# Other sources, orders and queues around the same matmuls: the first block's 1/rms from feature tiles, sums cast a step later, stores moved between two DMA queues

## The chip, the cores and the metric

The kernel runs on one core of one Trainium2 chip. The metric is the device time of one execution in microseconds (us); the time of a kernel is the median of its runs. TensorE is called PE, VectorE DVE, ScalarE ACT, GpSimd POOL, and SyncE, which here only starts transfers, SP.

## The reference

One layer of a hybrid network runs over 2048 prompt tokens and 64 sample tokens, 2112 rows of 1024 features in fp32. Cut to what matters here:

```
h    = rms_norm(x, g_pre)
vA, bA, cA, zA, q, f, iv, zB, gA, gB = split(h @ w_in)            # ten blocks of 1024 columns
yA   = (silu(zA) * bA * conv3(cA * vA)) @ w_a_out
o    = gated linear recurrence over q, f, iv, in chunks of 64 tokens, 8 heads
yB   = (rms_norm(o) * g_onorm * silu(zB)) @ w_b_out
x    = x + rms_norm((sigmoid(gA) * yA + sigmoid(gB) * yB) @ w_o, g_post)
x    = x + (p @ w_ple_proj) * sigmoid(rms_norm(x, g_ple) @ w_ple_gate)
```

`rms_norm(x, g)` is x / sqrt(mean(x*x) + 1e-6) * g over the 1024 features of a token. What the change calls W_G is `w_ple_gate`, and "ple" is the product of p (256 features) with `w_ple_proj`.

## The kernel before

**Tiles and products.** Features lie on the 128 partitions and tokens along the free dimension, so x comes as eight feature tiles `x_fm[k]` of 128 x 704. The tokens are done in three blocks of 704, each as two halves of 352 columns. Every fp32 product is made of three matmuls: each operand is split into a rounded part hi (a cast on ACT) and the rest lo (a subtraction on DVE) by `split` (L188), and hi*hi, hi*lo and lo*hi are added in PSUM. Most pairs of weight column blocks go through `sgroup`, which multiplies sums and differences of weight blocks (S1 to S4) with sums and differences of activation halves (T1 to T4), seven products (n = 0 to 6) in place of eight. `hook()` runs one queued step of other work after each product.

**The start (L1263 to L1370).** SP's queue asks for everything in this order: p of block 0, the ple weights (raws), the rows of block 0 as token tiles `x_tok` (twelve loads of 128 x 512), p of block 1, one feature tile of x, four weight tiles, the seven other feature tiles. ACT and DVE square and add up the twelve row tiles; GpSimd's power (L592) makes 1/rms, and six transposes (`spread`, L603) lay it out along the tokens as `rs`. PE meanwhile does block 0's ple, eight steps j of twelve matmuls (L1043 to L1045). Instructions are held in a written order by `behind_all` (behind named instructions on their engines) and `placed` (behind the last matmul).

Then `first_operands` (L702) makes the operands of block 0, one feature tile k at a time: `scaled_x` (L684, DVE) multiplies x by the gain and `rs`, `split` makes hi and lo, and from k = 4 on `sums_of` (L666) forms the four differences of the pair k-4, k (L670 to L673, DVE) and splits them at once into hi and lo. Two steps run ahead; the others are interleaved by `next_k` with block 1's ple (one step j, twelve matmuls, evacuated by ACT at L1050) and with the first `plain_group` (L432 to L434, twelve matmuls for each k). A second `plain_group` follows, whose weight splits are placed behind the entries of `summed`, and after it the first `sgroup` that needs the T sums.

**Stored sums.** A group's S sums and lo parts are made once (`combined`, L286), stored to DRAM by SP (`keep_sum` L276, `split_w` L225), and loaded again by the later blocks (L198, L219). Two groups are not formed in block 0, because `plain_group` did their columns there: FF/QQ of head 0 and the last GB group. They are formed at the start of block 1, and their sums stored by SP as well. The tag `s` has three buffers, which hold both new sums and some reloaded lo parts (`low_tile`).

**Heads.** `path_b` does a head with two `sgroup`s (FF/QQ and ZB/IV), and from the second head on with one gate group behind them; the head's attention steps are then put in the list of hooks and run within the next groups. For head 0 of block 0 there is no gate group, so its hooks start with the next product.

**The end.** In the last block `final_norm` runs once for each half, as hooks within the last product. It loads x again by GpSimd (`fetch`, L1176), two tiles ahead, normalizes (L1185, L1186), squares on ACT (L637), adds up on DVE (L638); the column sums are matmuls with ones (L619). The gate product of block 1 (`final_gate` with W_G, L528 to L530) was postponed into the last block and runs there in the same stretch; it reloads x and p by GpSimd (L1066), multiplies and adds (L1219, L1220) and stores y by GpSimd (L1221).

Of the kernel before, what the change touches and what calls it, by code (L numbers as in the profile page):

```python
# [10 lines left out]
F32 = mybir.dt.float32  # L11
# [71 lines left out]
def hybrid_step(  # L83
# [126 lines left out]
    def sum_tile(dt=F32):  # L210
        return wp.tile([P, 4, P], dt, tag="s", name=nm("s"), bufs=3)

    def split_w(raw, key=None):

        hi = wp.tile([P, 4, P], F32R, tag="hi", name=nm("hi"))
        if key in lows:
            lo = low_tile()
            A.copy(hi, raw)  # L218
            SP.dma_start(lo.bitcast(F32), lows[key])  # L219
            return hi, lo  # L220
        lo = wp.tile([P, 4, P], F32R, tag="lo", name=nm("lo"))
        split(raw, hi, lo)
        if key is not None:
            lows[key] = dram.tile([P, 4, P], F32, tag=f"lo{key}", name=nm("low"), bufs=1)
            SP.dma_start(lows[key], lo.bitcast(F32))  # L225
        return hi, lo

    def load_w(idx, anew=False):
# [41 lines left out]

    sums = {}

    def keep_sum(name, i1, s):

        sums.setdefault(i1, {})[name] = dram.tile([P, 4, P], F32, tag=f"{name}_{i1}", name=nm(name), bufs=1)
        SP.dma_start(sums[i1][name], s)  # L276
        return split_w(s, (i1, name))

    def kept_w(i1, i2, name, anew=False):

# [4 lines left out]

    def combined(i1, i2, first):  # L286

        with tc.high_priority():
            if not first:
                return {n: kept_w(i1, i2, n) for _, n, _, _, _ in PRODUCTS}  # L290
            a11, a21, a22, a12 = (load_raw(w_blk[i, h]) for i, h in ((i1, 0), (i2, 0), (i2, 1), (i1, 1)))
            out = dict(A11=split_w(a11, (i1, 0)))

            def total(name, x, y, op):
                s = sum_tile()
                V.tensor_tensor(s, x, y, op)
                out[name] = keep_sum(name, i1, s)
# [5 lines left out]
            out["A12"] = split_w(a12, (i1, 1))  # L303
            out["A22"] = split_w(a22, (i2, 1))
            total("S4", a12, s2, ALU.subtract)
            return out

# [40 lines left out]
    def sgroup(i1, i2, hc, sink, first, mid=None, by_k=False):  # L348


        w = combined(i1, i2, first or i1 not in sums)
        ps, got = {}, {}

        def product(n, ks):
            bank, block, operand, start, _ = PRODUCTS[n]
            if bank not in ps:
                ps[bank] = ps_gemm()
            hi, lo = w[block]
            for k in ks:
                xhi, xlo = hc[operand][k]  # L360
                add = partial(T.matmul, ps[bank], skip_group_check=not start)
                add(hi[:, k, :], xhi, start=start and k == 0, stop=False)  # L362
                add(hi[:, k, :], xlo, start=False, stop=False)  # L363
                last[0] = add(lo[:, k, :], xhi, start=False, stop=k == KH - 1).ins  # L364

        if by_k:
            for k in range(KH):
                for n in range(4):
                    product(n, (k,))
        for n, (bank, _, _, _, stop) in enumerate(PRODUCTS):  # L370
            if n >= 4 or not by_k:
                product(n, range(KH))
            if not stop:
                got[n] = hf()
                with tc.high_priority():
                    copied = A.copy(got[n], ps[bank])  # L376
                copies[0] = copied.ins
                if n == 2 and mid is not None:
                    mid(copied.ins)
            if n == 3:  # L380
                u2 = got[0]
                adds[0] = V.tensor_tensor(u2, u2, ps["b"], ALU.add).ins
            elif n == 4:
                sink(0, 0, ps["a"], None)
            elif n == 5:
                sink(1, 0, u2, ps["c"])
                adds[0] = V.tensor_tensor(got[1], got[1], got[2], ALU.add).ins
                sink(1, 1, u2, got[1])
# [313 lines left out]
    def first_operands(hc, rs, xs, hs):  # L702


        ends = []
        for k in range(KB):
            with behind_all(ends[k - 2][1:] if k >= 2 else ()):
                scaled_x(xs[k], k, rs)
# [4 lines left out]
            else:  # L713
# [285 lines left out]
    def path_b(bl, hc, first, kept, fills, hs):  # L999
# [6 lines left out]
        for hd in range(NH):  # L1006
# [157 lines left out]
    def final_norm(bl, segs, xo, acc, h2, kept, raw=False):  # L1164
# [10 lines left out]
                xks.append(rt())  # L1175
                G.dma_start(xks[j][:, c], x_fm[j * P : (j + 1) * P, segs[0]["t0"] : segs[0]["t0"] + n])  # L1176

        for _ in range(2 if bl["last"] else 4):
            fetch()
        copy = V.tensor_copy if bl["last"] else A.copy  # L1180
        yield from rms(acc, rs, segs, copy)
# [23 lines left out]
                h2[j] = None  # L1205
            yield

    def final_gate(bl, segs, h2, kept):
        def fetch(j):
            return [reload(kept[kind, j]) for kind in "xp"] if j < KB else None  # L1210

# [1 line left out]
        for j in range(KB):  # L1213
# [4 lines left out]
                A.activation(t[:, cols_of(s)], ps, AF.Sigmoid)  # L1218
            V.tensor_tensor(t, pj, t, ALU.mult)  # L1219
            V.tensor_tensor(t, t, xj, ALU.add)  # L1220
            G.dma_start(y_fm[j * P : (j + 1) * P, bl["t0"] : bl["t0"] + BN], t)  # L1221
            yield

    def rows_again(kept, h2):
# [42 lines left out]
    with tc.high_priority():  # L1267
        ph0 = load_p(blocks[0], SP)
        raws = [rt(4 * P).rearrange("p (j k c) -> p j k c", j=2, c=P) for _ in range(KH)]
        raws = [raw[:, j] for raw in raws for j in range(2)]  # L1270
        rows, xs, w1 = [], [], {}
        places = [(s["t0"] + o, q * 512) for s in blocks[0]["segs"] for _, o in tiles_of(HN) for q in range(2)]

        def ask_ple(*js):
            for j in js:
                SP.dma_start(raws[j], w_ple[j])

        def ask_rows(n):
            for r, c in places[len(rows) : len(rows) + n]:
                rows.append(rt(512))  # L1280
                SP.dma_start(rows[-1], x_tok[r : r + P, c : c + 512])

        def ask_x(n):
            for k in range(len(xs), len(xs) + n):
# [16 lines left out]
        ask_x(7)  # L1301
        held = []

        def held_split(j):
# [14 lines left out]
    ss = small.tile([P, 2, 6], F32, tag="rows", name="rows", bufs=1)  # L1319
    for n in range(4):  # L1320
        with behind_all(done):
            for i in range(3 * n, 3 * n + 3):
                t, total = rows[i], ss[:, i % 2, i // 2 : i // 2 + 1]
                if i % 3 == 2:
                    V.tensor_tensor(t, t, t, ALU.mult)
                    V.tensor_reduce(total, t, axis=mybir.AxisListType.X, op=ALU.add)
                else:
                    A.activation(t, t, AF.Square, accum_out=total)
            if n == 3:
                V.tensor_tensor(ss[:, 0, :], ss[:, 0, :], ss[:, 1, :], ALU.add)  # L1330
                done = [*done, rstd_of(ss[:, 0, :], ss[:, 0, :], 1.0 / D)]
# [10 lines left out]
    for _ in range(2):  # L1342
        with placed():
            run(first_ple, 1)
# [25 lines left out]
    for bi, bl in enumerate(blocks):  # L1370
# [125 lines left out]
```

## Time and profile before

| | |
|---|---|
| median of 3 runs | 2632.4 us (2630.19 to 2634.68) |
| the profiled execution | 2636.6 us; its span 2634.9 us |
| busy, share of the span | PE 99%, DVE 63%, ACT 58%, POOL 15% |
| mean granted PE clock | 0.995 |
| moved by DMA | 749.14 MB, mean 284 GB/s |

The span runs from the first to the last instruction, and 1.7 us of the execution lie around it. Times within the trace are counted from the span's start. In a row of the timeline stand the start, the duration, the engine, the line, the operation, result and operands, the shapes and a count; in brackets the engine's idle time before it and what ended that. The granted clock is a share of full speed.

### The profile page before, as it was taken

Reading aid. Unit: us, or ns where it says so; the run is one execution under the profiler, and the core shown is the slowest. Engines: PE = TensorE matmul, PEld = TensorE weight load, DVE = VectorE, ACT = ScalarE, POOL = GpSimd, SP = SyncE. Lnnn points to the kernel's source line nnn. Section 1 sums busy time; section 2 is a strip of 40 time slices with the busy share of each in tenths; the row PEclk is TensorE's granted clock in tenths of the full one; section 3 lists DMA queues with packets and bytes.
Section 4 is the critical chain, followed back from the end, with each engine's and each line's share of the span. In section 5 each row is a group of like instructions: output and inputs, shape, how many; then the busy total and the mean of one; then the engine's idle time right before and its main releaser. Section 6 shows DMA issues by size and latency. Waiting matters only on the chain.

```text
span 2634.9 us, 47400 instructions
## 1 busy us (share of the span) xinstructions
PE 2600.3 (99%) x16550; PEld 2582.7 (98%) x16550; DVE 1666.3 (63%) x3233; ACT 1538.5 (58%) x2948; POOL 386.9 (15%) x713
## 2 busy tenths in 40 slices
PE   7999999999999999999999999999999999999999
PEld 7999999999999999999999999999999999999998
DVE  7687887898777555455545568553455544479656
ACT  5666666554334644677745556466667745565636
POOL 1000000200432210011112211021000101210220
PEclk9999999999999999999999999999999999999999
DMA  8678778898988997767789989599777789989967
GB/s 290 220 262 283 246 269 278 298 316 291 332 299 283 350 328 257 244 224 226 223 288 358 386 306 313 187 363 346 230 228 222 223 258 345 379 308 308 329 234 240
DMA packets 364912, 749.14 MB, mean 284 GB/s; under 512 B 44832, under 2 KB 49472, under 8 KB 364672
## 3 DMA queue, kind: packets, MB, share of 16 engines
q1 hardware_dynamic: 322560, 584.00, 65.2%
q0 software_dynamic: 41824, 162.06, 16.8%
q8 instruction: 130, 2.13, 0.3%
q14 instruction: 110, 0.90, 0.1%
q10 hardware_dynamic: 288, 0.05, 0.0%
HBM read 534.88 MB, written 211.04 MB: 283 GB/s over the span
## 4 chain that ended last, share of the span: by engine, by line
PE 92%; DMA 3%; DVE 2%; issue 1%; ACT 1%; POOL 0%; SPq 0%; ACTq 0%; DVEq 0%; POOLq 0%
PE pg L362 19%; PE pg L364 19%; PE pg L363 19%; PE pg L529 5%; PE pg L530 5%; PE pg L528 5%; PE pg L495 4%; PE pg L496 4%; PE pg L497 4%; PE pa L980 1%; PE pa L944 1%; PE pa L982 1%; PE pa L930 1%; DMA raw<-S 1%; DMA r<-x_fm 1%
## 5 line engine op out<-in xcount | busy, mean ns | idle before, releaser
L362 PE MATMUL pg<-r,hi 128*128 128x352 f32 x3304 | 1094.8, 331 | 4.2 <-DVE r L408 2.6
L363 PE MATMUL pg<-r,hi 128*128 128x352 f32 x3304 | 1068.0, 323 | 0.0
L364 PE MATMUL pg<-r,lo 128*128 128x352 f32 x2356 | 763.2, 324 | 2.2 <-DMA lo<-low 2.2
L218 ACT CAST hi<-raw 128x512 fp32r<-128x512 f32 x720 | 444.3, 619 | 498.8 <-PE pg L363 167.3
L362 PEld LDWEIGHTS pg<-r,hi 128*128 128x128 f32 x3304 | 623.0, 189 | 9.0 <-DVE r L408 4.0
L363 PEld LDWEIGHTS pg<-r,hi 128*128 128x128 f32 x3304 | 623.3, 189 | 0.0
L364 PEld LDWEIGHTS pg<-r,lo 128*128 128x128 f32 x2356 | 443.6, 188 | 2.9 <-DMA lo<-low 2.8
L364 PE MATMUL pg<-r,s 128*128 128x352 f32 x948 | 307.2, 324 | 0.0
L529 PE MATMUL pg<-r,hi 128*128 128x352 f32 x768 | 249.5, 325 | 0.0
L528 PE MATMUL pg<-r,hi 128*128 128x352 f32 x768 | 249.3, 325 | 0.1
L188 ACT CAST hi<-raw 128x512 fp32r<-128x512 f32 x218 | 134.3, 620 | 152.9 <-PE pg L363 46.1
L188 DVE TENSOR_TENSOR r<-r,r 128x352 fp32r<-128x352 f32 (+3 forms) x298 | 183.1, 636 | 63.8 <-ACT r L188 62.9
L496 PE MATMUL pg<-r,hi 128*128 128x352 f32 x672 | 217.3, 325 | 0.0
L495 PE MATMUL pg<-r,hi 128*128 128x352 f32 x672 | 213.6, 325 | 0.1
L530 PE MATMUL pg<-r,lo 128*128 128x352 f32 x656 | 213.0, 325 | 0.0
L188 ACT CAST r<-r 128x352 fp32r<-128x352 f32 (+3 forms) x298 | 161.9, 578 | 61.9 <-DVE r L671 17.4
L188 DVE TENSOR_TENSOR lo<-raw,hi 128x512 fp32r<-128x512 f32 x218 | 149.3, 686 | 68.1 <-ACT hi L188 59.3
L364 PEld LDWEIGHTS pg<-r,s 128*128 128x128 f32 x948 | 178.6, 188 | 0.0
L188 ACT CAST hi<-s 128x512 fp32r<-128x512 f32 x160 | 98.1, 619 | 123.8 <-PE pg L363 112.8
L376 ACT COPY hf<-pg 128x352 f32<-128x352 f32 x354 | 157.0, 446 | 12.2 <-PE pg L364 11.6
L529 PEld LDWEIGHTS pg<-r,hi 128*128 128x128 f32 x768 | 145.2, 189 | 0.4 <-DVE r L188 0.3
L528 PEld LDWEIGHTS pg<-r,hi 128*128 128x128 f32 x768 | 145.1, 189 | 0.4 <-ACT r L188 0.4
(372 smaller groups left out, 4160.5 us busy)
## 6 DMA issues: line engine op xcount, KB each, us to landing
raw<-w_blk SPq DMA_DIRECT2D x570, 256.0 KB, 4.2
lo<-low SPq DMA_DIRECT2D x411, 256.0 KB, 4.4
raw<-S SPq DMA_DIRECT2D x408, 256.0 KB, 4.4
low<-lo SPq DMA_DIRECT2D x322, 256.0 KB, 3.7
s<-low SPq DMA_DIRECT2D x309, 256.0 KB, 4.2
S<-s SPq DMA_DIRECT2D x160, 256.0 KB, 3.1
r<-w_blk POOLq DMA_DIRECT2D x64, 256.0 KB, 7.2
S<-r POOLq DMA_DIRECT2D x64, 256.0 KB, 5.9
```

What stands on the lines that cost most here:

```text
L188: return A.copy(hi, src).ins, V.tensor_tensor(lo, src, hi.bitcast(F32), ALU.subtract).ins
L218: A.copy(hi, raw)
L362: add(hi[:, k, :], xhi, start=start and k == 0, stop=False)
L363: add(hi[:, k, :], xlo, start=False, stop=False)
L364: last[0] = add(lo[:, k, :], xhi, start=False, stop=k == KH - 1).ins
L376: copied = A.copy(got[n], ps[bank])
L495: add(hi[:, k, :], xhi, start=start and k == 0, stop=False)
L496: add(hi[:, k, :], xlo, start=False, stop=False)
L497: last[0] = add(lo[:, k, :], xhi, start=False, stop=k == KH - 1).ins
L528: T.matmul(ps, hi[:, k % 4, :], xhi[:, c], start=k == ks[0], stop=False)
L529: T.matmul(ps, hi[:, k % 4, :], xlo[:, c], start=False, stop=False)
L530: last[0] = T.matmul(ps, lo[:, k % 4, :], xhi[:, c], start=False, stop=k == ks[-1]).ins
```

## The change

Six things change. (1) Block 0's rows are not loaded as token tiles any more. SP's order is p, two ple weights, two tiles of x, and so on, then p of block 1 and the four weight tiles. ACT squares the eight feature tiles, DVE adds them up, and the sums over the partitions are six matmuls with ones (`col_rstd`), as in the later norms. (2) `sums_of` is cut in two: a pair's differences are formed in its own step, behind the split of that step's x, and their casts are made one step later, with a last step for the last pair. (3) The hooks of head 0 in block 0 start three products later. (4) The sums that block 1 forms are stored by GpSimd in place of SP. (5) The last block's `final_norm` loads x three tiles ahead in place of two. (6) The postponed W_G product stores y by SP in place of GpSimd.

```
-    def split_w(raw, key=None):
+    def split_w(raw, key=None, queue=SP):
...
-            SP.dma_start(lows[key], lo.bitcast(F32))
+            queue.dma_start(lows[key], lo.bitcast(F32))
...
-    def keep_sum(name, i1, s):
+    def keep_sum(name, i1, s, queue):
...
-        SP.dma_start(sums[i1][name], s)
-        return split_w(s, (i1, name))
+        queue.dma_start(sums[i1][name], s)
+        return split_w(s, (i1, name), queue)
...
     def combined(i1, i2, first):
+        queue = SP if first else G
         with tc.high_priority():
-            if not first:
+            if not first and i1 in sums:
...
     def sums_of(hc, pair):
+        return split_sums(hc, *add_sums(pair))
+
+    def add_sums(pair):
         (b11, b12), (b21, b22) = ([half(x, h) for h in range(2)] for x in pair)
         s, t = rt(), rt()
...
+        return s, t
+
+    def split_sums(hc, s, t):
         hi, lo = split_rt(s)
...
     def first_operands(hc, rs, xs, hs):
-        ends = []
+        ends, added = [], []
...
-                summed.append(sums_of(hc, (xs[k - KH], xs[k])))
+                with behind_all(ends[k]):
+                    if added:
+                        summed.append(split_sums(hc, *added.pop()))
+                    added.append(add_sums((xs[k - KH], xs[k])))
             yield
+        summed.append(split_sums(hc, *added.pop()))
+        yield
...
             attn = [head_attn(i, gs, d, hd) for i, gs in enumerate(bl["parts"])]
+            hooks.extend([None] * 3 if first and hd == 0 else [])
...
-        for _ in range(2 if bl["last"] else 4):
+        for _ in range(3 if bl["last"] else 4):
             fetch()
...
-    def final_gate(bl, segs, h2, kept):
+    def final_gate(bl, segs, h2, kept, queue=G):
...
-            G.dma_start(y_fm[j * P : (j + 1) * P, bl["t0"] : bl["t0"] + BN], t)
+            queue.dma_start(y_fm[j * P : (j + 1) * P, bl["t0"] : bl["t0"] + BN], t)
...
-        ask_ple(0, 1, 2, 3)
-        ask_rows(8)
+        ask_ple(0, 1)
+        ask_x(2)
+        ask_ple(2, 3)
+        ask_x(2)
         ask_ple(4, 5)
-        ask_rows(4)
+        ask_x(2)
         ask_ple(6, 7)
+        ask_x(2)
         ph1 = load_p(blocks[1], SP)
-        ask_x(1)
         ask_w(0)
         ask_w(1)
-        ask_x(7)
...
+    acc, rs = rt(), rt()
+
+    def add_square(k):
+        sq = rt() if k else acc
+        ends = [A.activation(sq, xs[k], AF.Square).ins]
+        if k:
+            ends.append(V.tensor_tensor(acc, acc, sq, ALU.add).ins)
+        return ends
+
+    for n, ks in enumerate(((0,), (1, 2), (3, 4), (5,), (6,), (7,))):
         with behind_all(done):
...
+            for k in ks:
+                done = add_square(k)
         with placed():
             run(first_ple, 1)
         with behind_all(done):
-            for j in (n + 2,) if n < 3 else (5, 6, 7):
-                done = held_split(j)
+            done = held_split(n + 2)
...
     with behind_all((*done, *copies)):
+        cols = [col_rstd(half(acc, h), HN) for h in range(2)]
         ph, done = split_p(ph1)
-    for _ in range(2):
-        with placed():
-            run(first_ple, 1)
+    with placed():
+        run(first_ple, 1)
     with behind_all(done):
-        rs = rt()
-        cols = [spread(ss[:, 0, 3 * h : 3 * h + 3], HN) for h in range(2)]
+        cols = [spread(col, HN) for col in cols]
...
-            for j, _ in enumerate(final_gate(blocks[bi - 1], segs, rows2, kepts[bi - 1])):
+            for j, _ in enumerate(final_gate(blocks[bi - 1], segs, rows2, kepts[bi - 1], SP)):
```

More of the change, by code (lines that the diff above doesn't have):

```diff
@@ L286, in combined @@
     def combined(i1, i2, first):
+        queue = SP if first else G
         with tc.high_priority():
-            if not first:
+            if not first and i1 in sums:
                 return {n: kept_w(i1, i2, n) for _, n, _, _, _ in PRODUCTS}
             a11, a21, a22, a12 = (load_raw(w_blk[i, h]) for i, h in ((i1, 0), (i2, 0), (i2, 1), (i1, 1)))
-            out = dict(A11=split_w(a11, (i1, 0)))
+            out = dict(A11=split_w(a11, (i1, 0), queue))
             def total(name, x, y, op):
@@ L296, in total @@
                 V.tensor_tensor(s, x, y, op)
-                out[name] = keep_sum(name, i1, s)
+                out[name] = keep_sum(name, i1, s, queue)
                 return s
@@ L302, in combined @@
             s2 = total("S2", s1, a11, ALU.subtract)
-            out["A12"] = split_w(a12, (i1, 1))
-            out["A22"] = split_w(a22, (i2, 1))
+            out["A12"] = split_w(a12, (i1, 1), queue)
+            out["A22"] = split_w(a22, (i2, 1), queue)
             total("S4", a12, s2, ALU.subtract)
@@ L348, in sgroup @@
     def sgroup(i1, i2, hc, sink, first, mid=None, by_k=False):
-        w = combined(i1, i2, first or i1 not in sums)
+        w = combined(i1, i2, first)
         ps, got = {}, {}
@@ L1270, in hybrid_step @@
         raws = [raw[:, j] for raw in raws for j in range(2)]
-        rows, xs, w1 = [], [], {}
-        places = [(s["t0"] + o, q * 512) for s in blocks[0]["segs"] for _, o in tiles_of(HN) for q in range(2)]
+        xs, w1 = [], {}
         def ask_ple(*js):
@@ L1276, in ask_ple @@
                 SP.dma_start(raws[j], w_ple[j])
[L1278 to L1281, printed above, removed]
         def ask_x(n):
@@ L1317, in hybrid_step @@
     first_ple = ple(blocks[0], ph, kepts[0], held, True)
-    ss = small.tile([P, 2, 6], F32, tag="rows", name="rows", bufs=1)
-    for n in range(4):
-        with behind_all(done):
[L1322 to L1331, printed above, removed]
+    acc, rs = rt(), rt()
[6 more added lines that the diff above has]
+    for n, ks in enumerate(((0,), (1, 2), (3, 4), (5,), (6,), (7,))):
+        with behind_all(done):
+            for k in ks:
+                done = add_square(k)
         with placed():
@@ L1334, in hybrid_step @@
         with behind_all(done):
-            for j in (n + 2,) if n < 3 else (5, 6, 7):
-                done = held_split(j)
-    for _ in range(2):
-        with placed():
-            run(first_ple, 1)
+            done = held_split(n + 2)
     with behind_all((*done, *copies)):
+        cols = [col_rstd(half(acc, h), HN) for h in range(2)]
         ph, done = split_p(ph1)
-    for _ in range(2):
-        with placed():
-            run(first_ple, 1)
+    with placed():
+        run(first_ple, 1)
     with behind_all(done):
-        rs = rt()
-        cols = [spread(ss[:, 0, 3 * h : 3 * h + 3], HN) for h in range(2)]
+        cols = [spread(col, HN) for col in cols]
         done = A.copy(half(rs, 0), cols[0]).ins, V.tensor_copy(half(rs, 1), cols[1]).ins
```

## The prediction

> **What bounds the kernel now.** I read the page, then PE's own waits, then the timeline around each of them, because with PE at 99% a change can only win where PE stands still or runs slow.
>
> ```profile
> span 2634.9 us, 47400 instructions
> PE 2600.3 (99%) x16550; PEld 2582.7 (98%) x16550; DVE 1666.3 (63%) x3233; ACT 1538.5 (58%) x2948; POOL 386.9 (15%) x713
> ```
> ```profile
> PE pa L1043 <- ACT r L188: 6.6, 1, 6.6
> PE pa L619 <- DVE r L638: 5.2, 2, 4.8
> PE pg L433 <- DVE r L188: 4.3, 1, 4.3
> PE pa L1043 <- ACT r L1050: 4.0, 3, 1.8
> ```
>
> PE idles only 34.6 us (2634.9 less 2600.3). The columns here are the total in us, the times and the longest. The first 6.6 us stand before the first matmul. The three others lie where the change works: the first block's operands (4.3 and 4.0) and the norm near the end (4.8 of the 5.2); two smaller ones, at head 0 and at block 1's first sums, come with their parts below. A wait costs more than its length, as the granted clock shows in the stretches behind them (start and end, length, the busy time of PE, PE's weight loads, DVE, ACT and POOL with their counts, the granted clock, DMA's share and GB/s):
>
> ```profile
> 28.66:72.54 43.88, 35.45 (x184) 33.50 (x183) 32.41 (x52) 21.32 (x41) 4.55 (x9) 0.88 0.70 256
> 34.08:40.90 6.82, 6.82 (x23) 6.36 (x24) 6.82 (x13) 3.12 (x9) 0.54 (x1) 0.52 0.92 341
> 1055.50:1061.20 5.70, 3.67 (x14) 3.49 (x13) 0.16 (x1) 2.54 (x4) 0.00 (x0) 0.70 0.82 285
> 2527.30:2538.60 11.30, 6.55 (x25) 6.40 (x25) 6.37 (x11) 1.72 (x4) 5.75 (x9) 0.72 0.49 163
> ```
>
> ```profile
> 41.05 0.33 PE L433 MATMUL pg<-r,hi 128*128 128x352 f32 x1
> 41.21 0.32 PE L434 MATMUL pg<-r,lo 128*128 128x352 f32 x1
> ```
>
> At full clock a 352-column matmul starts every 0.16 us (41.05 to 41.21; I use 0.161); at 0.52 the 23 matmuls of 34.08 to 40.90 take 0.29 each. The waits and this slow clock together are the stock that the change can win.
>
> **Part 1 and 2, the start.** PE's stage of interleaved ple and plain products runs from 28.66 to 72.54, 43.88 us, and holds 184 matmuls, which at 0.161 need 29.6. So 14.3 us are lost there. The first piece is the wait of 4.3 and the slow clock behind it. Its rows are the transposes that spread `rs`, DVE's first two scalings, and from the chain of waits the landing of the last row tile:
>
> ```profile
> 25.93 0.82 PE L603 MATMUL pa<-ident,rows 128*128 128x128 f32 x6
> ```
> ```profile
> 27.41 0.95 DVE L684 SCALAR_TENSOR_TENSOR r<-r,vec,r 128x704 f32<-128x704 f32 x1
> 32.64 0.95 DVE L684 SCALAR_TENSOR_TENSOR r<-r,vec,r 128x704 f32<-128x704 f32 x1 [4.28 <-DMA r<-x_fm]
> ```
> ```profile
> 12.36 4.73 DMA r<-x_tok
> ```
>
> `rs` is there at 27.4, but the second x tile, which stood behind the rows and the weights in SP's queue, lands only at 32.6 (4.28 us of DVE's time), and the first tile's lo stands behind its scaling in DVE's queue. With x ahead that wait is gone. What is late next is `rs` itself, since it needs all of x:
>
> ```profile
> r<-x_tok SPq DMA_DIRECT2D x12, 256.0 KB, 5.2
> r<-x_fm SPq DMA_DIRECT2D x8, 352.0 KB, 11.7
> ```
> ```profile
> 871.52 1.72 POOL L592 TENSOR_TENSOR cols<-cols,mhalf 128x3 f32<-128x3 f32 x2 [17.84 <-DVE cols L590]
> ```
> ```profile
> 2501.89 0.72 PE L619 MATMUL pa<-ones,r 128*128 128x1 f32 x6
> ```
> ```profile
> L188 DVE TENSOR_TENSOR r<-r,r 128x704 fp32r<-128x704 f32 x10 | 8.9, 887 | 1.8 <-ACT r L188 1.6
> L684 DVE SCALAR_TENSOR_TENSOR r<-r,vec,r 128x704 f32<-128x704 f32 x8 | 7.5, 946 | 4.4 <-DMA r<-x_fm 4.3
> L188 DVE TENSOR_TENSOR lo<-raw,hi 128x512 fp32r<-128x512 f32 x6 | 4.0, 683 | 0.0
> L188 DVE TENSOR_TENSOR r<-r,r 128x352 fp32r<-128x352 f32 x8 | 3.8, 517 | 0.0
> ```
>
> A p tile has x's shape (352 KB), a ple tile 128 x 256 numbers (128 KB). Up to the last row tile stood 2 p, 6 ple and 12 row loads in SP's queue, 4544 KB; up to the last x tile will stand 2 p, 8 ple and 8 x, also 4544 KB. So the last x lands where the last row tile did, at 12.36 + 4.73 = 17.1. Its square takes at most about 0.8 and its addition 0.89 (an 887 ns form): the sum stands at about 19. Earlier squares and additions, 0.8 and 0.89 each, lie beside the ple and wait for data. PE ends ple step 5 two steps (24 x 0.161 = 3.9) ahead of 25.93, at 22.1: three us to spare. Then the column sums (0.72), two powers (1.72) and about 0.4 of hand-overs end at 24.9, beside step 6, which ends at 24.8; the six transposes (0.82 busy, 0.7 to the next start) end at 25.7, a copy makes `rs` at 26.3. PE goes on with ple step 7 and block 1's step 0 (24 x 0.161) until 29.6, 0.9 later than now. By then DVE has scaled two tiles (2 x 0.95) and split one (2 x 0.52): 29.3. No wait is left.
>
> After this DVE must stay ahead. Up to the last tile's lo it has 8 scalings (7.6), 4 pairs and 4 whole lo parts (4.1 + 3.5), 3 sets of four differences (12 x 0.52 = 6.2), by the later casts only two sets of two (3.5), and 4 weight splits (2.7): 27.6, so 53.9. PE reaches that tile's products after 7 + 7 steps of 12 matmuls, 168 x 0.161 = 27.0, at 56.6. PE is then the bound by 2.7 us, and the last pair's casts go beside the second plain group. In the old order the third cast set (1.8) and two further weight splits (1.4) stand ahead of that lo and would leave no margin. The stage ends at 29.6 + 180 x 0.161 = 58.6 in place of 72.5: 13.9 us. But there is this:
>
> ```profile
> 65.50 0.43 PE L1043 MATMUL pa<-r,r 128*128 128x352 f32 x1 [1.83 <-ACT r L1050]
> ```
>
> There, and twice before (4.0 us in all), PE waits for ACT to evacuate the ple, while ACT's queue is held by casts whose differences DVE hasn't made. Casts a step later find them ready, but ACT still waits for scalings; I leave one such wait, 1.6. **Part 1 and 2: -12.3**, between -6 (only the x wait of 4.3 and some slow clock go) and -14.3.
>
> A rule beside it: the Trainium skill ("TensorE: Matmul & The Clock Gate", Part 1) has PE at half clock until a window of about 3.4 us was busy, so at most 1.7 us for a wait. The row of 34.08 shows 6.82 us at 0.52, two such windows; by the rule this stage would give 1.4 us less, and the measured row decides.
>
> **Part 3, head 0's hooks.**
>
> ```profile
> 106.75 0.44 PE L913 MATMUL pa<-ident,r 128*128 128x128 f32 x2 [1.38 <-DVE r L408]
> ```
>
> The transposes of v stand in PE's queue before DVE has made v. Three products later (36 x 0.161 = 5.8 us) v is there; the 17 steps fit the 21 hooks of three groups. **-1.4**, between 0 and -1.5.
>
> **Part 4, block 1's sums stored by GpSimd.**
>
> ```profile
> 1057.71 0.66 PE L364 MATMUL pg<-r,lo 128*128 128x352 f32 x1 [2.04 <-DMA lo<-low]
> ```
> ```profile
> SPq L225 <- DVE lo L188: 6.5, 5, 3.5
> SPq L219 <- DMA low<-lo: 5.0, 2, 2.7
> ```
> ```profile
> S<-s SPq DMA_DIRECT2D x160, 256.0 KB, 3.1
> ...
> S<-r POOLq DMA_DIRECT2D x64, 256.0 KB, 5.9
> ```
>
> Stretch 1055.50 to 1061.20 holds 14 matmuls, 2.25 us of its 5.70, so up to 3.5 hang on that late load. SP's queue there waits 6.5 us in all for DVE to finish what it must store, with weight loads behind; on GpSimd's queue these waits (16 stores) hold nothing that PE needs soon. Against it, a store lands 5.9 after GpSimd's issue in place of 3.1 after SP's, and SP's loads already wait 5.0 (twice) for a store to free a buffer; 2.8 more at each of eight sums would be +22 if nothing hid it. I take **-2.0**, near the upper row, since only two of SP's waits there are for a stored buffer.
>
> **Part 5 and 6, the end.**
>
> ```profile
> DVE r L1186 <- DMA r<-x_fm: 5.2, 2, 2.8
> ```
> ```profile
> 2519.24 0.55 POOL L1221 DMA_DIRECT2D y_fm<-r  x1 [6.45 <-issue]
> 2519.78 1.09 POOL L1176 DMA_DIRECT2D r<-x_fm  x2
> ```
> ```profile
> 2532.16 1.27 PE pa L619 x6
> ```
>
> A circle: GpSimd holds x's loads behind a y store, which waits for DVE, which waits for x. DVE stands for 5.2 us in two waits, PE for 4.8. With y on SP and x one tile earlier both DVE waits go, and the column sums of 2532.16 come 5.2 earlier, at 2527.0, when PE is about there. Of the 11.30 us of 2527.30 to 2538.60, 19 large matmuls and six small need 3.1 + 0.7: 7.5 are lost. I take **-6.8**, between -2 (GpSimd then waits for buffers) and -7.5. SP now waits for DVE's y, but is far ahead:
>
> ```profile
> 2517.16 0.33 SPq L198 DMA_DIRECT2D raw<-w_blk  x1
> ```
> ```profile
> 2558.86 0.46 ACT L1218 ACTIVATE r<-pg 128x352 f32<-128x352 f32 x1
> ```
>
> W_G's last weight load leaves at 2517 and its last gate, whose product uses it, is taken at 2559. A column block is 48 matmuls, 7.7 us, so the load leaves about four of them ahead of its use: some 30 us cover such waits.
>
> **The sum.** -12.3 - 1.4 - 2.0 - 6.8 = -22.5: 2636.6 becomes 2614.1. That execution is 4.2 above the median of 2632.4, so the median becomes 2609.9, **2610**. Elsewhere PE stays at 99% and later work shifts whole.
>
> **Rivals.** (a) *ACT and DVE stay the start's bound*: the start gives 6, the rest 10.2: 2616. For it: DVE has only 2.7 us to spare; against: the first 4.3 of wait has one cause. (b) *x is late at the end all the same*, since the third tile waits for a buffer: 2.0 in place of 6.8, so 2615. For it: GpSimd's wait of 6.45 is named "issue"; against: DVE's addition precedes that store. (c) *The sums' stores hold block 1* and it ends slower. The eight sums sit in three buffers; GpSimd's queue is not empty:
>
> ```profile
> 1014.84 0.55 POOL L1221 DMA_DIRECT2D y_fm<-r  x1 [7.66 <-DVE r L1220]
> ```
>
> A sum stored behind such a y store is late by 7.66 + 2.8 = 10.5; three buffers cover three products of 12 matmuls, 5.8; 4.7 reach PE, with some 1.6 of slow clock 6.3, eight times 50: 2632.4 - 20.5 + 50 = 2662. It decides from 2.6 us for each sum (20.5 / 8). Against: the second group's stores meet an idle GpSimd. The Trainium skill ("SBUF — State Buffer", SBUF: two separate sides) speaks for (c): DVE's two-port operations lock GpSimd out while it writes descriptors. The row of 1014.84 shows an issue of 0.55 all the same, so no run here shows that lock. (d) *Nothing reaches PE*, as new waits replace the old: 2628 to 2632.
>
> **Chances.** Forecast (2604 to 2613) 0.52, (a) 0.17, (b) 0.11, both together (2621) 0.06, (c) 0.06, (d) 0.05, above the forecast's best 0.03. The range 2603 to 2622 holds the first four. A measurement can tell 0.2%, 5.3 us: faster 0.89, same 0.05, slower 0.06.
>
> **What would show it.** Right: no PE wait near 4.3 behind 28, the stage's last L434 at about 59, no waits of L1186 for x_fm, L619 without a wait near the end, no L913 wait in head 0. Wrong: PE idle at L603 for more than 1 us (x lands late), new waits for `lo` or `s` at the start of block 1, a stage that still ends behind 65.

## The result, and the profile after

| | before | after |
|---|---|---|
| median of the runs beside each other, us | 2631.6 (2630.2 to 2634.7, 4 runs) | 2611.6 (2609.6 to 2612.7, 4 runs) |
| profiled execution, us | 2636.6 | 2611.6 |
| its span, us | 2634.9 | 2609.9 |
| mean granted clock | 0.995 | 1.000 |

The ratio after to before is 0.9921, with a 95% interval of 0.9909 to 0.9933: the change takes off 20 us, more than the 5.3 us that can be told. The prediction was 2610, its range 2603 to 2622. The two profiled executions differ by 25.0 and not by 20, because that of before lay 4 to 5 us above its median and that of after on it.

The head of the page and PE's own waits (total in us, times, longest), after:

```profile
span 2609.9 us, 47443 instructions
...
PE 2588.6 (99%) x16562; PEld 2572.5 (99%) x16562; DVE 1667.1 (64%) x3232; ACT 1538.9 (59%) x2940; POOL 392.6 (15%) x722
```
```profile
PE pa L1058 <- ACT r L188: 6.6, 1, 6.6
PE pg L363 <- DVE r L409: 3.1, 9, 0.6
PE pa L1008 <- DVE r L1003: 1.7, 1, 1.7
PE pg L363 <- ACT hi L218: 1.5, 2, 0.7
PE pg L365 <- DMA lo<-low: 1.2, 1, 1.2
PE pa L1058 <- ACT r L1065: 0.9, 2, 0.6
```

PE now idles 21.3 us in place of 34.6, and 6.6 of that still stand before the first matmul. Of the four longest waits of before the three others are gone or small: nothing of 4.3 behind 28 us, 0.9 in place of 4.0 for the ple's evacuation (L1058, L1043 before), no column sums among the waits. Nor is there slow clock left: the mean of 0.995 in before stands mostly for five stretches at half clock (from 33.8, 54.2, 1057.8, 1771.1 and 2532.3), 23.9 us in all, and after has none before its last matmuls. The line numbers have moved: L1008, the transposes of head 0's normed output (its product is L1003), is new among the waits; L365 is L364 of before.

The start, in two views: the timeline, then the stretch from the second ple's first step to the stage's end (the columns as in the prediction):

```profile
19.79 0.89 DVE L1336 TENSOR_TENSOR r<-r,r 128x704 f32<-128x704 f32 x1 [0.17 <-ACT r L1334]
...
21.00 1.39 PE L620 MATMUL pa<-ones,r 128*128 128x1 f32 x12
...
24.27 0.88 PE L604 MATMUL pa<-ident,cols 128*128 128x128 f32 x6
...
25.80 1.81 DVE L693 SCALAR_TENSOR_TENSOR r<-r,vec,r 128x704 f32<-128x704 f32 x2
...
32.80 0.43 PE L1058 MATMUL pa<-r,r 128*128 128x352 f32 x1 [0.63 <-ACT r L1065]
```
```profile
28.90:59.70 30.80, 29.93 (x184) 29.10 (x183) 29.80 (x49) 19.67 (x38) 4.55 (x9) 1.00 0.60 207
```

The column sums run at 21.0 and the transposes at 24.3, 1.1 and 0.6 us ahead of the forecast; the first two scalings follow one another at 25.80 and nobody waits for x. But the last addition (L1336) ends only at 20.7: of the three microseconds to spare that the prediction saw ahead of the column sums, 0.3 were there. The 184 matmuls that took 43.88 us take 30.80 at full clock. ACT's first gate begins at 59.57:

```profile
58.28 1.28 ACT L744 ACT_TABLE_LOAD   x1
59.57 0.47 ACT L744 ACTIVATE r<-pg 128x352 f32<-128x352 f32 x1
```

The table load ahead of it is a good mark for the stage's end: in before it stood at 71.12.

Comparing when the same matmul of the sequence starts in the two traces gives the gain place by place, as a median over each stretch (times of before):

| stretch of before, us | after is ahead by, us | step |
|---|---|---|
| 74 to 86 | 12.8 | start: +12.8 |
| 150 to 180 | 12.7 | head 0: -0.1 |
| 880 to 900 | 12.5 | -0.2 |
| 920 to 940 | 11.0 | a wait at 898 of after: -1.4 |
| 1066 to 1080 | 14.9 | block 1's sums: +3.9 |
| 1755 to 1765 | 14.7 | -0.2 |
| 1776 to 1800 | 17.4 | column sums of the second block: +2.7 |
| 2518 to 2526 | 16.8 | -0.6 |
| 2542 to 2560 | 24.6 | the last block's column sums: +7.8 |
| 2600 to 2620 | 24.8 | end |

Three of these places in the trace of after: block 1 (the matmuls where before waited 2.04), the last column sums, and the new wait with the stretch around it.

```profile
1043.00:1049.00 6.00, 6.00 (x40) 6.00 (x39) 1.54 (x3) 4.44 (x7) 0.54 (x1) 1.00 0.97 318
```
```profile
2509.59 0.80 PE L620 MATMUL pa<-ones,r 128*128 128x1 f32 x6
```
```profile
899.31 0.43 PE L365 MATMUL pg<-r,lo 128*128 128x352 f32 x1 [1.19 <-DMA lo<-low]
```
```profile
895.00:900.00 5.00, 3.81 (x24) 3.52 (x23) 1.98 (x3) 1.85 (x4) 0.00 (x0) 1.00 1.02 406
```

The first stretch holds 40 matmuls in 6 us with no idle time; the last column sums carry no bracket, so PE did not stand. In the last stretch the 16 DMA engines are full (a share of 1.02, 406 GB/s), and a low part comes 1.19 late.

And head 0, where a wait was traded: the wait of 1.38 at the transposes of v is gone, and this one is new:

```profile
124.25 0.69 DVE L1003 TENSOR_TENSOR r<-pa,ms 128x512 f32<-128x512 f32 x1
```
```profile
125.08 0.63 PE L1008 MATMUL pa<-ident,r 128*128 128x128 f32 x4 [1.70 <-DVE r L1003]
```

### The profile page after: what moved, and what is told of

Its sections match the earlier page's. It is cut to its first block, busy times and chain, and to the rows that moved or that the text cites. A ratio compares the mean times of both kernels' runs of the same rounds, so it can differ in the third digit from the quotient of the medians.

```text
span 2609.9 us, 47443 instructions
## 1 busy us (share of the span) xinstructions
PE 2588.6 (99%) x16562; PEld 2572.5 (99%) x16562; DVE 1667.1 (64%) x3232; ACT 1538.9 (59%) x2940; POOL 392.6 (15%) x722
## 4 chain that ended last, share of the span: by engine, by line
PE 89%; DMA 3%; DVE 2%; issue 2%; ACT 1%; POOL 1%; DVEq 0%; POOLq 0%; ACTq 0%; SPq 0%
PE pg L363 19%; PE pg L365 19%; PE pg L364 19%; PE pg L496 4%; PE pg L497 4%; PE pg L498 4%; PE pg L530 4%; PE pg L531 4%; PE pg L529 4%; PE pa L994 1%; PE pa L958 1%; PE pa L996 1%; PE pa L944 1%; DMA r<-w_blk 1%; DMA raw<-S 1%
## 5 line engine op out<-in xcount | busy, mean ns | idle before, releaser
L363 PE MATMUL pg<-r,hi 128*128 128x352 f32 x3304 | 1092.9, 331 | 4.6 <-DVE r L409 3.1
L364 PE MATMUL pg<-r,hi 128*128 128x352 f32 x3304 | 1067.6, 323 | 0.0
L365 PE MATMUL pg<-r,lo 128*128 128x352 f32 x2356 | 762.1, 323 | 1.2 <-DMA lo<-low 1.2
L363 PEld LDWEIGHTS pg<-r,hi 128*128 128x128 f32 x3304 | 622.2, 188 | 9.1 <-DVE r L409 3.2
L364 PEld LDWEIGHTS pg<-r,hi 128*128 128x128 f32 x3304 | 622.2, 188 | 0.0
L365 PEld LDWEIGHTS pg<-r,lo 128*128 128x128 f32 x2356 | 442.3, 188 | 1.8 <-DMA lo<-low 1.7
L365 PE MATMUL pg<-r,s 128*128 128x352 f32 x948 | 306.2, 323 | 0.1
L365 PEld LDWEIGHTS pg<-r,s 128*128 128x128 f32 x948 | 178.4, 188 | 0.4 <-DMA s<-low 0.4
```

## The experiments

All kernels below differ from the changed kernel by the lines shown. Their medians stand beside those of before on the same chip. A difference of one or two microseconds between medians is hardly more than their spread, so each verdict rests on the place in the trace that the edit touches.

**Old order of loads at the start (part 1 undone).** The lines of before for the loads, the row squares and the ple's first steps, with the new `first_operands` (only the order of the loads is shown, cut to one line each):

```
-ask_ple(0, 1); ask_x(2); ask_ple(2, 3); ask_x(2) ...
+ask_ple(0, 1, 2, 3); ask_rows(8); ask_ple(4, 5); ask_rows(4) ... ask_x(1); ask_w(0); ask_w(1); ask_x(7)
```

> The changed kernel, but block 0's 1/rms is again made from row tiles loaded ahead of x; the casts of the operand sums stay a step later. Theory (x ahead carries most of the start's 13.0 us): PE waits again for the second x tile, 4.3 us and the slow clock behind it, the stage ends at 68 to 72 in place of 59.6, and the time is 2611.6 + 9 = 2620 to 2624. Rival (the late casts carry it, since ACT and DVE bound the stage): only the 4.3 us and 3 of slow clock come back early, DVE then catches up, the stage ends near 64 and the time is 2615 to 2617.

Measured: 2614.1 (2613.3 to 2616.2) beside 2632.8, ratio 0.993 (0.9917 to 0.9942). The timeline:

```profile
31.45 0.95 DVE L693 SCALAR_TENSOR_TENSOR r<-r,vec,r 128x704 f32<-128x704 f32 x1 [3.05 <-DMA r<-x_fm]
```
```profile
32.88 1.10 PE L434 MATMUL pg<-r,hi 128*128 128x352 f32 x2 [3.11 <-DVE r L188]
```

DVE waits for the second x tile again, PE for DVE, and the clock is half until 38.0 (its rows stand in the last section). But no wait for the evacuations comes behind, and the table load at the stage's end stands at 63.28, 5.0 behind that of after and 7.8 ahead of that of before, so the stage ends at 64.6. The theory was wrong and the rival right on the stage: x ahead is worth 5.0 on top of the late casts. In the medians less shows, some 2.5: PE is 5.0 behind after until 180 us, but 2.4 at 902 to 1080, mostly because this execution has no wait at 898.

**Casts at once (part 2 undone).**

```
-with behind_all(ends[k]):
-    if added:
-        summed.append(split_sums(hc, *added.pop()))
-    added.append(add_sums((xs[k - KH], xs[k])))
+summed.append(sums_of(hc, (xs[k - KH], xs[k])))
```

> The changed kernel, but the casts of an operand sum follow its differences at once, as before. Theory (x ahead carries most): at most 3 us come back, as PE's waits for the evacuation of the ple on ACT (1.8 us at a time); 2612 to 2614.6. Rival (by the prediction's own working, no margin is left without the later casts: 1.8 of casts and 1.4 of weight splits stand ahead of the last lo): two or three such waits with slow clock behind them, the stage ends at 64 to 66, 2616 to 2618.

Measured: 2617.3 (2617.1 to 2617.9) beside 2632.8, ratio 0.9942 (0.9929 to 0.9954).

```profile
47.15 0.66 PE L1053 MATMUL pa<-r,r 128*128 128x352 f32 x1 [1.94 <-ACT r L1060]
...
53.23 0.43 PE L1053 MATMUL pa<-r,r 128*128 128x352 f32 x1 [0.41 <-ACT r L1060]
...
59.15 0.43 PE L1053 MATMUL pa<-r,r 128*128 128x352 f32 x1 [1.77 <-ACT r L1060]
```

(L1053 and L1060 are L1058 and L1065 of after.) With x ahead and the casts at once, the evacuation comes late three times, and the table load stands at 64.73: 6.4 us back, of which 0.6 stood already at 20 to 27 us. This is the rival too, and the working that gave the old order no margin. So by the table load the late casts are worth 6.4 beside x ahead, and 7.8 (71.12 - 63.28) without it; x ahead 5.0 and 6.4 (71.12 - 64.73), each to about half a microsecond, by which the starts of two executions of one kernel differ. The two halves nearly add up to the 12.8.

**No empty hooks (part 3 undone).**

```
-hooks.extend([None] * 3 if first and hd == 0 else [])
```

> The changed kernel without the three empty hooks ahead of head 0. Theory (the hooks traded one wait for another): PE's wait of 1.4 us at the transposes of v comes back near 93 to 94 us, and the waits of 1.70 and 0.29 us at the transposes of the normed output near 123 go; 2611.3 to 2611.6, no difference that can be told. Rival (the prediction: the hooks gain 1.4 and the waits at 123 have another cause and stay): 2613.0.

Measured: 2610.9 (2610.5 to 2613.6) beside 2632.8, ratio 0.9919 (0.9905 to 0.9933).

```profile
PE pa L927 <- DVE r L409: 1.4, 1, 1.4
```
```profile
112.71 0.69 DVE L1003 TENSOR_TENSOR r<-pa,ms 128x512 f32<-128x512 f32 x1 [1.15 <-POOL ms L593]
```
```profile
110.04 0.60 ACT L1000 ACTIVATE r<-pa 128x512 f32<-128x512 f32 x1 [0.51 <-PE pa L996]
```

The old wait is back (L927 is L913 of before), that of L1008 is gone. From 131 us on PE runs 0.3 ahead of after, but 0.25 of it stands already at 65 to 85, so the hooks cost 0.1, as the table has it. Without them ACT waits for head 0's output and squares it (L1000) as soon as PE has made it, at 110.04, and DVE's product begins 2.7 us later. With them, in the trace of after, PE has made it at 114.4, and ACT has the next head's activations (L855 to L859) ahead of the square:

```profile
118.10 0.79 ACT L859 ACTIVATE r<-r 128x704 f32<-128x704 f32 x1
...
119.99 0.60 ACT L1000 ACTIVATE r<-pa 128x512 f32<-128x512 f32 x1
```

The square comes 5.5 us behind PE, and DVE, which has the next head's scaling and weight sums in its queue, begins the product 4.3 after that. So the wait is named for DVE, but most of the lateness arises on ACT. The hooks moved a wait.

**Block 1's sums stored by SP (part 4 undone).**

```
-queue = SP if first else G
+queue = SP
```

> The changed kernel with block 1's new sums and low parts stored by SP again. Theory (16 stores of late DVE results hold SP's weight loads): a wait for a low part of about 2 us with 1.6 of slow clock comes back near 1043, and 2611.6 becomes 2613.6 to 2615.5; the wait of 1.2 us at 898, 80 us ahead of the first of these stores, is still there. Rival (that load was late by its place in time alone): 2611.6 and no wait near 1043.

Measured: 2616.4 (2614.5 to 2619.7) beside 2632.8, ratio 0.9938 (0.9925 to 0.995).

```profile
895.47 0.43 PE L365 MATMUL pg<-r,s 128*128 128x352 f32 x1 [0.32 <-DMA s<-low]
...
898.06 0.43 PE L365 MATMUL pg<-r,lo 128*128 128x352 f32 x1 [0.40 <-DMA lo<-low]
...
1045.13 0.43 PE L365 MATMUL pg<-r,lo 128*128 128x352 f32 x1 [1.58 <-DMA lo<-low]
```

The late low part is back where the theory put it, 1.58 long, and PE loses 1.9 us between 913 and 1045. No slow clock follows, so in this trace it costs half of what before paid there; of the wait at 898 two short ones are left. The median is above what the theory expected, and by the ratios 4.5 behind that of after. But the execution profiled is the fastest of the five, and its trace ends 1.2 behind after; what cost the others up to 5 us more no trace shows.

**Two tiles of x ahead at the end (part 5 undone).**

```
-for _ in range(3 if bl["last"] else 4):
+for _ in range(2 if bl["last"] else 4):
```

> The changed kernel with x fetched two tiles ahead at the end, as before; y stays on SP. Theory (the circle is broken by either half; what held x's loads was the y store ahead of them in GpSimd's queue): at most 2 us come back, 2611.6 to 2613.6, and DVE's waits for x stay under 1 us each. Rival (the depth of the fetch is what counts): DVE's two waits of 2.4 to 2.8 us come back, PE waits about 4 us at the column sums and runs slowly behind them, 2617 to 2619.

Measured: 2610.4 (2609.4 to 2611.2) beside 2629.8, ratio 0.9925 (0.9912 to 0.9937). DVE's waits for x from 2460 to 2530 and the column sums:

```profile
DVE r L1201 <- DMA r<-x_fm: 0.2, 1, 0.2
```
```profile
2508.92 0.80 PE L620 MATMUL pa<-ones,r 128*128 128x1 f32 x6
```

Nothing comes back: with y on SP, two tiles ahead are enough.

**y stored by GpSimd (part 6 undone).**

```
-final_gate(blocks[bi - 1], segs, rows2, kepts[bi - 1], SP)
+final_gate(blocks[bi - 1], segs, rows2, kepts[bi - 1])
```

> The changed kernel with the postponed gates' y stored by GpSimd again; x stays three ahead. Theory (y's place in GpSimd's queue is the cause): x's loads stand behind a y store again, DVE waits for x for 2 us or more, PE waits at the column sums near 2510, and 5 to 7.5 us come back: 2616.6 to 2619. Rival (one more tile ahead covers the same wait): 2611.6 to 2612.6.

Measured: 2616.0 (2614.2 to 2616.7) beside 2629.8, ratio 0.9944 (0.9932 to 0.9956). GpSimd's queue, DVE's waits, PE:

```profile
2499.70 0.54 POOL L1236 DMA_DIRECT2D y_fm<-r  x1 [3.20 <-ACT hi L218]
2500.23 0.54 POOL L1191 DMA_DIRECT2D r<-x_fm  x1
```
```profile
DVE r L1201 <- DMA r<-x_fm: 2.7, 2, 2.2
```
```profile
2512.91 0.80 PE L620 MATMUL pa<-ones,r 128*128 128x1 f32 x6 [3.69 <-DVE r L639]
```
```profile
2514.02:2517.41 3.39, 3.39 (x13) 3.39 (x12) 1.59 (x2) 0.00 (x0) 2.61 (x4) 0.50 0.81 256
```

The old order stands again: the load of x follows a y store that waited 3.20, DVE waits 2.7 for x, PE 3.69 at the column sums and then runs at half clock for 3.4 us, and from there to the end PE is 5.0 further back than ahead of it. (The row of the y store names a cast on ACT; the product that it stores, DVE's L1235, ended at 2499.12. Ahead of it DVE was busy and did not wait for x, so here it is a chain and no circle.) Of the 7.8, y on SP alone gives all, and the third tile ahead alone 7.8 - 5.0 = 2.8: a wait of 3.69 in place of 4.8, and one stretch at half clock in place of two, which is 1.7.

**One more hook in head 0.**

```
 if step == 2:
-    hooks.append(None)
+    hooks.extend([None] * (2 if first and hd == 0 else 1))
```

> The changed kernel with one more empty hook in head 0, between the normed output's square and its transposes, so that these stand one product (12 matmuls, 1.9 us) later in PE's queue. Theory (the transposes come 1.70 us ahead of DVE's product): the waits of 1.70 and 0.29 us near 123 go and nothing replaces them: 2609.6. Rival (DVE and ACT are behind as a whole there, and the next step waits instead): 2611.6.

Measured: 2610.0 (2608.8 to 2611.1) beside 2629.8, ratio 0.9923 (0.991 to 0.9937). No wait of L1008 is left, and from 130 us on PE runs 2.1 ahead of after, 0.2 of it from the start; the rest is as the theory says. By the medians, on another chip than after's, 2 us cannot be told.

**All new sums and their low parts stored by GpSimd**, 160 and 274 of them by the trace (the expectation counted 314 low parts; SP keeps 48, of weights outside the sums).

```
-queue = SP if first else G
+queue = G
```

> The changed kernel with all new sums and low parts of block 0 stored by GpSimd too, 152 sums and 314 low parts in all, in place of 8 and 8. The price of a store on GpSimd's queue is thereby multiplied by some 20 to 30. Theory (a store that lands 2.6 us later, and waits in GpSimd's queue, is hidden while three buffers hold the sums): 2609 to 2617. Rival (the prediction's rival c: a late store holds the buffers of sums and low parts, and PE): from 0.5 us for each of 152 sums, 2680 and more, with PE waits for s and lo all over block 0.

Measured: 2609.4 (2608.8 to 2612.3) beside 2629.8, ratio 0.9923 (0.991 to 0.9937).

```profile
low<-lo POOLq DMA_DIRECT2D x274, 256.0 KB, 3.5
S<-s POOLq DMA_DIRECT2D x160, 256.0 KB, 3.4
```

The expectation's price for rival (c) falls. The sums land 3.4 us after their issue, against 3.2 for SP's 152 in after, the low parts 3.5, against 3.7 for SP's 314, and no wait for `s` or `lo` appears in block 0. The six waits of 0.25 us that after has there, one each 49 us from 180 to 425 (the row of L363 and L409), are gone too, with 0.5 us a head: the wait, and as much again because the matmuls behind it start further apart (0.27 in place of 0.16 for the first). Slow clock has no part in it, though the later expectation put it there; the granted clock of after is 1.00 from 130 to 860. One wait grew: L1008 in head 0, from 1.70 to 2.69. And one for `s`, of 1.17, stands at 1729, where after has none.

**The changed kernel again, and two versions on the same chip.** The first kernel is unaltered; the second stores all sums by GpSimd and has two more hooks ahead of head 0's second transposes; the third stores them so and has one hook ahead of head 0 in place of three.

```
 queue = G
-    hooks.append(None)
+    hooks.extend([None] * (3 if first and hd == 0 else 1))
```
```
 queue = G
-hooks.extend([None] * 3 if first and hd == 0 else [])
+hooks.extend([None] * 1 if first and hd == 0 else [])
```

> The changed kernel once more, unaltered, on the same chip as the next two. Theory (the wait of 1.2 us at 898 comes and goes, since the 16 DMA engines are full there, and five kernels with the same code up to that place have between 0 and 1.2 of it): its waits outside 880 to 910 are those of the first profiled execution within 0.3 us, the wait at 898 is under 0.8, and the time is 2609 to 2612. Rival (the wait belongs to the code): 1.0 to 1.3 us again at 898.

> The changed kernel with all new sums and low parts of block 0 stored by GpSimd, and two more empty hooks ahead of head 0's transposes of the normed output (these come 2.7 us too early with GpSimd's stores; two products are 3.9 us). Theory (both gains add up: six waits of 0.25 us with their slow clock, some 2.9, and the 1.7 to 2.0 at 123): 2611.6 - 4.5 = about 2607, no PE wait at the transposes, none over 0.3 us between 130 and 760. Rival (DVE and ACT stay behind and another step of head 0 waits): 2609.

> The changed kernel with all new sums and low parts of block 0 stored by GpSimd, and one empty hook ahead of head 0 in place of three. Theory (one product, 1.9 us, already covers the wait of 1.4 at the transposes of v, and the later transposes are then 3.9 us earlier, where DVE has less queued ahead of their product, as in the kernel without hooks): no wait at either, 2607. Rival (the wait at the second transposes grows with any delay of the first): 1 to 2 us there, 2609 to 2610.

Measured, beside 2631.1: 2610.4 (2609.5 to 2611.4), 2607.4 (2606.5 to 2608.8) and 2609.7 (2608.6 to 2610.2); ratios 0.9921, 0.9910 (0.9894 to 0.9927) and 0.9918. PE's waits in the unaltered kernel, then in the second version, then in the third:

```profile
125.64 0.63 PE L1008 MATMUL pa<-ident,r 128*128 128x128 f32 x4 [1.69 <-DVE r L1003]
...
899.24 0.43 PE L365 MATMUL pg<-r,lo 128*128 128x352 f32 x1 [0.77 <-DMA lo<-low]
```
```profile
130.01 0.30 PE L1008 MATMUL pa<-ident,one 128*128 128x128 f32 x1 [0.72 <-DVE one L1003]
```
```profile
94.28 0.87 PE L927 MATMUL pa<-ident,r 128*128 128x128 f32 x4 [0.88 <-DVE r L409]
...
132.78 0.30 PE L1008 MATMUL pa<-ident,lone 128*128 128x128 f32 x1 [1.97 <-DVE lone L1003]
```

The wait of head 0 repeats to 0.01 us; the one at 899 is 0.77 in place of 1.19. It is 0.58 with the later hook, two waits of 0.32 and 0.40 with the sums on SP, and absent without the hooks and in both experiments on the end, whose code is the same up to there as after's. So it comes and goes with the same code. That the full DMA engines decide it, as the theory had it, is argued and not shown. The second version beats both kernels: 3.0 us below the changed one on the same chip, all its runs below all of that one's. It was expected at 2607. What is left of its two hooks is a wait of 0.72 for another tile of the same product. The third met its rival: one hook still leaves 0.88 at v, and the second transposes wait for the last of the three parts.

## Why the prediction was right, step by step

**Part 1 and 2** (forecast -12.3): -12.8. The stage's end was put at 58.6, 60.2 with the one wait allowed, and came at 59.6, from a start 0.7 earlier than put. One term was read from half of what it stands for: the column sums were put at 0.72, a row of six matmuls for one half, and take 1.39 for both (twelve). Two evacuation waits of 0.87 together are left where one of 1.6 was allowed. The mechanism stands: the lower end of its bounds, -6 for x alone, is what the casts at once leave (-6.4), and the late casts bring the rest. The prediction gave no split; the split that I put to the first two experiments, x ahead carrying most, was wrong.

**Part 3** (-1.4): it cost 0.1, in the trace and by the experiment that undoes it. This is the step that failed. It took the wait's disappearance for the gain and asked only whether the 17 steps fit the 21 hooks. All later steps move by three products as well, and the normed output of head 0 lands behind the next head's work, in ACT's queue first and then in DVE's. The bounds, 0 to -1.5, held no loss, and no reason had excluded one.

**Part 4** (-2.0): -3.9 against the profiled execution of before, -1.9 in the trace with it undone, -4.5 by the medians. The wait is common to both traces (2.04 and 1.58). The rest of the difference is the slow clock, 1.7 us, which followed it in before and not in the experiment; the forecast left it out, and allowed for it in the bound of -3.5.

**Part 5 and 6** (-6.8): -7.8 in the trace. The circle is right for before and the column sums do not wait, but the credit was given to both edits, and y on SP has all of it. Undone, part 5 costs nothing.

**The rivals.** (a) and (b) did not come: the start gave 12.8, and DVE's waits for x near the end are gone. (c) was given 50 us for eight sums, from 7.66 us behind a y store and 2.8 of later landing each. In after the y stores among them wait 0.53 (at 1003.86 and 1011.66), and the eight sums land 4.3 us after their issue, 1.1 later than SP's; the 5.9 of the prediction's row belongs to other stores, `S<-r` from another stage. SP's loads do wait for stored buffers, as the rival had it: from 1000 to 1075 for sums as in the row below and 0.2 for low parts, in before 2.6 and 5.0. PE waits for none of it.

```profile
S<-s POOLq DMA_DIRECT2D x8, 256.0 KB, 4.3
```
```profile
SPq L219 <- DMA S<-s: 7.0, 3, 4.7
```

On the rule of the Trainium skill ("SBUF — State Buffer", SBUF: two separate sides), quoted for (c), the experiment has GpSimd issue 274 low parts in this row, from the groups of instructions (busy time, mean ns of one):

```profile
L225 POOL DMA_DIRECT2D low<-lo x274 | 149.3, 545 | 264.0 <-DVE lo L188 204.7
```

Its mean of 545 ns lies at the 0.54 to 0.55 of the single issues shown here, beside a DVE that is busy 64% of the span, so no lock shows here either. The row does not tell which of DVE's operations ran beside these issues, so it does not test the rule itself.

**The sum.** -22.5 was forecast against the profiled execution, and 25.0 came. By the table of stretches: 12.8 - 0.1 in place of 13.7 for the first three parts, 3.9 for 2.0, 7.8 for 6.8; steps that were not forecast are -1.4 at 898, +2.7 at the second block's column sums, and -1.0 in all from the small ones. The 2.7 are a short wait in before, and 1.7 of slow clock behind it, from 1771.1 to 1774.5:

```profile
1768.54 1.47 PE L619 MATMUL pa<-ones,r 128*128 128x1 f32 x12 [0.47 <-DVE r L638]
```

After has the same sums without a wait, and the unaltered second execution a wait of 0.16 at full clock. Whether the change or chance took this one away stays open, as only one execution of before is profiled. Seen as PE's own time, it idles 13.3 us less, and the five stretches at half clock had cost half of their 23.9, 11.9 us: nearly half of the gain is the clock.

Against the median the gain is 20.0 where 22.5 was forecast; 2611.6 for 2610. That it came so near is in part luck: parts that were forecast too high and too low offset each other, and the losses were all read from one execution of before that had more slow clock than others have. Its mean clock is 0.995, and that of the 25 runs of before beside the experiments 0.996 to 0.998. A thousandth of the span is 2.6 us, so by these rounded means two thousandths would account for its 4 to 5 us above the median (an estimate; no other execution of before is profiled).

## What to carry to other kernels

When PE's queue is moved against those of ACT and DVE, ask of every later step of the chain, not only of the first, what stands ahead of it in each other queue at its new time. When two edits break one circle, undo each alone before crediting both: here one queue entry did all, and the extra buffer nothing. Take a transfer's price from a row of the same tile shape and the same stretch: a row of other stores and the wait of one y store made a harmless move of sixteen stores look like 50 us, and 434 on that queue cost nothing that shows.

## What was not expected of the hardware

The clock after a wait does not go by the wait's length. In all these traces it changes only at the borders of equal stretches of 3.41 us (between its changes in before lie 2, 4, 1, 293, 1, 208, 1, 222 and 2 of them), and within one it is 1.00 or 0.50; a mean such as 0.70 mixes the two. The rows lie just within such stretches: in before around the wait of 0.47, in the first experiment around its wait of 3.11, in the fourth around that of 1.58. The number behind PE's busy time counts the matmuls, with those that only reach into the stretch; of the first row's 23, twelve are column sums.

```profile
1767.73:1771.12 3.39, 2.92 (x23) 2.65 (x22) 0.99 (x3) 2.53 (x6) 2.04 (x3) 1.00 1.05 398
1771.15:1774.54 3.39, 3.39 (x14) 3.39 (x13) 0.53 (x1) 0.97 (x2) 0.18 (x1) 0.50 1.04 400
```
```profile
27.79:31.19 3.40, 1.91 (x9) 1.18 (x7) 0.61 (x1) 2.13 (x5) 0.00 (x0) 1.00 1.02 406
31.21:34.60 3.39, 1.72 (x4) 1.25 (x5) 3.15 (x6) 0.87 (x2) 0.00 (x0) 0.50 1.03 412
34.62:38.02 3.40, 3.40 (x13) 3.40 (x13) 3.40 (x7) 1.78 (x5) 0.00 (x0) 0.50 1.05 397
```
```profile
1041.40:1044.80 3.40, 2.14 (x14) 1.86 (x12) 0.98 (x2) 2.07 (x3) 0.00 (x0) 1.00 0.94 296
```

In every stretch it follows how many matmuls began in the one before, column sums left out. A full stretch begins 21. In the thirteen traces, up to the last matmul, 9,874 stretches lie. Eleven of them begin nine or fewer, and each of these is followed by one at half clock; the others begin ten or more, and none of them is. At half clock a busy PE begins 11 or more, so one busy stretch brings the full clock back, and a second slow one comes only where PE stood or did column sums in the first: here from 31.2, with four begun, in the prediction's row of 34.08, with nine, and in before at 2532.3, with eight. So 0.47 us of waiting, with twelve column sums behind it, cost 1.7 us of clock, as 1.94 did in the second experiment and 3.69 in the sixth, and the waits of 1.70 in after and 1.58 in the fourth, with twelve or more matmuls begun in each stretch that they touch, cost none. A trace can lack some records of matmuls, so the border between nine and ten is one of these traces alone; why the clock goes by it they do not tell.

The Trainium skill ("TensorE: Matmul & The Clock Gate", Part 1) has the full clock come back after at least one busy window of about 3.4 us, and calls the window free-running. The stretches here agree with both, the two at half clock in the first experiment included.
